# The head of a two-layer diffusion step: another order for its loads, its statistics and its first weight tiles

## The chip, the cores and the metric

The kernel runs on one core of a Trainium2 chip. Five engines work side by side, each with its own queue in program order: TensorE (PE; its weight loads are shown apart as PEld), VectorE (DVE), ScalarE (ACT), GpSimd (POOL) and SyncE (SP), which issues every DMA here. The metric is the device time of one execution in microseconds (us), the median of several runs; the profile and the trace come from one further execution.

## The reference

Two groups of 128 tokens (context and latent) of width 1024 go through the same two layers. Each layer is a half-step feed-forward, a token mixer and another half-step feed-forward. What matters here is the start of the first one, where for each group a conditioning vector gives a shift and a scale:

```
mod = silu(cond) @ w_ada[l] + b_ada[l]          # 9 vectors of 1024: shift, scale, gate, ...
h   = rmsnorm(x, g[0]) * (1 + mod[1]) + mod[0]  # rmsnorm: x * rsqrt(mean(x*x) + eps) * g
g, u = split(h @ ffn_w_in[l, 0], 2)             # 1024 -> 2 x 2816
x   = x + 0.5 * mod[2] * ((silu(g) * u) @ ffn_w_out[l, 0])
```

Everything is computed to nearly fp32 accuracy.

## The kernel before

**Layout.** Activations lie transposed: 8 slices of 128 channels (`KD` = 8) by 256 tokens (`NT`, both groups). A matrix product of fp32 accuracy is made from three faster ones: each weight tile and each operand is split into a rounded high part and the rest, and `mm3` adds high x high, high x rest and rest x high. A weight tile is 128 x 1024 fp32 (0.52 MB) in HBM, loaded into one of four `raw` buffers; `emit_hi` (ScalarE, a cast) and `emit_lo` (VectorE, a subtraction) split it; the load that reuses its buffer waits for `emit_lo`. The first five tiles (`T0` = 5) put their parts into the general `big` buffers (25 of them), the later ones into five `wh` and five `wl`. A weight tile times 8 operands is 24 products.

**The operand.** The normalisation's 1/rms is a factor per token, so it is left to the evacuation of the products (`rb`, a row of 1/rms on all partitions). The operand of slice m (`feed["hs"][m]`, here *operand m*) is x times `Amod` (gain times 1 + scale; `xfeed`: two ScalarE instructions, then two on VectorE for the rest), and two further columns hold the shift: 258 columns.

**The head.** These are all instructions ahead of the loop over tiles in `ffn_in`, at the end of `backbone`. The queues are in the order of the program text; nothing reorders them. Shift and scale of slice b need *block b* of `w_ada`: 1024 x 256 fp32, two DMAs of 0.52 MB. `block_mm(b)` multiplies it with silu(cond) into the one `pa` accumulator (8 products, 16 records), and VectorE copies that out. `block_feed(b)` (here *feed b*) transposes the copy by two small fp32 products with a selector, computes shift, scale and `Amod` on VectorE, and calls `xfeed(b)`. In a loop of ten steps, step s does block s, feed s-1, and the products of operands up to s-2 with the prepared tiles that have joined:

```
for t in range(T0):
    if step < max(2, JOIN[t]):
        continue
...
    while done[t] <= step - 2:
        k = done[t]
        mm3(pre[t], ws[t][k:k + 1], feed["hs"][k:k + 1], k == 0, k == KD - 1)
        done[t] += 1
```

Ahead of the loop x is squared slice by slice on ScalarE (`xstat`), VectorE adds the squares up in `sqa`, and `norm_chain` makes `rb`: a product with ones, a multiply-add (`rsv`), a power on GpSimd (`rsr`), a diagonal matrix on VectorE, a product with ones, a copy. Tiles 0 to 2 use the three main accumulators (`pm`), tiles 3 and 4 the two halves of `spare`. The sixth tile of the weight stream is the first that `ffn_in` multiplies itself; it takes the accumulator of tile 0, the seventh that of tile 1, once VectorE has evacuated them into `wide`.

**Loads.** SP issues in program order: the conditioning vectors, x (1.05 MB), constants (0.13 MB), parameters (0.14 MB), then weight tiles and blocks in turn. A DMA whose buffer is still read waits in SP's queue, and all behind it with it.

**Order further on.** The wrappers of the engines keep a rough clock for each (`Pace`), by which the side work of later stages (adaLN streams, attention, scans) is put between the products. In the head no such choice is made but for the norm's chain.

Of the kernel before, what the change touches and what calls it, by code (L numbers as in the profile page):

```python
# [13 lines left out]
ALU = mybir.AluOpType  # L14
# [26 lines left out]

ADA_DEPTH = 2
T0 = 5
JOIN = (0, 0, 3, 4, 5)
RAW_BUFS = 4
WH_BUFS = 5
WL_BUFS = 5
# [30 lines left out]
BR_LESS = (0, 0, 0, 0, 1, 1, 1, 1)  # L78
WO_LESS = (0, 0, 0, 0, 1, 1, 1, 1)
FO_LESS = (0, 0, 0, 0, 1, 1, 1)  # L80
LOADS = (2, 3, 4, 4)
PRE = 2
AHEAD = ("", "hl", "h", "lh", "")
T_SIDE = 3
T_SETUP = 6
YCUT = ((0, 2), (2, 2), (4, 2), (6, 2))
# [338 lines left out]
def backbone(ctx: ExitStack, tc: tile.TileContext, seq, wst, wada, wa0, wrow, xT_d, cT_d, cB_d, ck_d, cv_d, h0_d, prm_d, cst_d,  # L425
# [71 lines left out]
    def C(name):  # L497
        return cst[:, CST[name][0]:CST[name][1]]
# [59 lines left out]
    def misc(gen):  # L558
        add(gen, True)
# [5 lines left out]
    def load(out, src):  # L565
        nc.sync.dma_start(out=out, in_=src)
        pace.op("dma", out.free_size() * P * 4 / 360e3, [out], [])
# [215 lines left out]
    def rstd_diag(acc, scale, more=None):  # L783
        ps = ps1(2)
        for g in range(2):
            T_.matmul(ps[:, g:g + 1], lhsT=acc[:, g * P:(g + 1) * P], rhs=C("ones")[:, 0:1], start=True,
                      stop=more is None)
            if more is not None:
                T_.matmul(ps[:, g:g + 1], lhsT=more[:, g * P:(g + 1) * P], rhs=C("ones")[:, 0:1], start=False, stop=True)
        r = rstd_cols(ps, 2, scale)  # L790
        drop("s1", ps)
        dg = t1k()
        for g in range(2):
            V.tensor_scalar(out=dg[:, g * P:(g + 1) * P], in0=C("ident"), scalar1=r[:, g:g + 1], scalar2=None, op0=ALU.mult)
        return dg
# [867 lines left out]
    def ssd_norm(l, yv, yh, yl, box):  # L1663
# [25 lines left out]
            V.scalar_tensor_tensor(out=box["ts"][m], in0=box["ts"][m], scalar=1.0, in1=rb[:, :NT], op0=ALU.add, op1=ALU.mult)  # L1689
        box["done"] = True  # L1690

    load(cT, cT_d)
    load(x, xT_d)
    load(cst[:, 0:CST_E], cst_d[:, 0:CST_E])
    load(prm[0], prm_d[0, :, 0:PRM_R])
    V.memset(silc, 0.0)
    V.memset(halfc, -0.5)
    S.activation(out=silc[:, :, 0:2], in_=cT, func=AF.Silu)
    blocks = []

    def block_load():
        blocks.append([big(), big()])
# [3 lines left out]
    def split():  # L1706
        emit_hi()
        emit_lo()

    for n in LOADS[:-1]:  # L1710
        load_more(n)
        block_load()
    load_more(LOADS[-1])
    feed_open(0, 0)
    for m in range(KD):
        xstat(m)()
    box = {"rb": None}
    misc(norm_chain(box))
    split()
    split()  # L1720
    settle(lambda: box["rb"] is not None)
    evs = {}

    def block_mm(b):
        ps = pada()
        for k in range(KD):
            j = k % 4
            T_.matmul(ps[32 * j:32 * j + 32, :], lhsT=silc[:, k, :], rhs=blocks[b][k // 4][:, j * NT:(j + 1) * NT],
                      start=(k < 4), stop=(k >= 4))
        evs[b] = t1k()  # L1730
        V.tensor_copy(evs[b], ps)
        blocks[b] = None

    def block_feed(b):
        ev = evs.pop(b)
        pt = ps1(4)
        for h in range(2):
            T_.matmul(pt[:, 2 * h:2 * h + 2], lhsT=ev[:, h * P:(h + 1) * P], rhs=C("sel"), start=True, stop=True)
        sc = mods[0][:, 1, b, :]
        V.tensor_scalar(out=sc, in0=pt[:, 0:2], scalar1=R(0, "bada")[:, KD + b:KD + b + 1], scalar2=1.0, op0=ALU.add,  # L1740
                        op1=ALU.add)
        sh = mods[0][:, 0, b, :]
        V.tensor_scalar(out=sh, in0=pt[:, 2:4], scalar1=R(0, "bada")[:, b:b + 1], scalar2=None, op0=ALU.add)
        drop("s1", pt)
        V.tensor_scalar(out=Amod[0][:, 0, b, :], in0=sc, scalar1=R(0, "gain")[:, b:b + 1], scalar2=None, op0=ALU.mult)
        hi, lo = feed["hs"][b]
        V.tensor_copy(hi[:, NT:], sh)
        V.tensor_tensor(out=lo[:, NT:], in0=sh, in1=hi[:, NT:], op=ALU.subtract)
        xfeed(b)()

    spare = ps2()
    pre, ws = [], []
    done = {}
    for step in range(KD + 2):
        if step < KD:
            block_mm(step)
            if len(blocks) < KD:
                block_load()
                if len(blocks) == KD:
                    st["cap"] = len(seq)  # L1760
                    load_more(st["lo"] + RAW_BUFS)
        if 1 <= step <= KD:
            block_feed(step - 1)
        for t in range(T0):
            if step < max(2, JOIN[t]):
                continue
            if t == len(pre):
                ws.append(tiles8(use(("fin", 0, 0, (t % 2) * KF + t // 2))))
                pre.append(pmain(NT + 2) if t < 3 else spare[:, t - 3, 0:NT + 2])
                done[t] = 0  # L1770
            while done[t] <= step - 2:
                k = done[t]
                mm3(pre[t], ws[t][k:k + 1], feed["hs"][k:k + 1], k == 0, k == KD - 1)
                done[t] += 1
        if st["lo"] < T0 and step + 2 >= JOIN[st["lo"]]:
            split()
        if step >= KD - 3:
            for what in AHEAD[step - KD + 3]:
                what = emit_hi() if what == "h" else emit_lo()
    while st["lo"] < T0 + PRE:  # L1780
        if st["hi"] == st["lo"]:
            emit_hi()
# [54 lines left out]
```

## Time and profile before

| | |
|---|---|
| median of 3 runs | 1553.76 us (1552.73 to 1557.59) |
| profiled execution | 1555.05 us, of which the span is 1553.2 us |
| TensorE busy | 1513.9 us (97%) |
| VectorE, ScalarE, GpSimd busy | 1303.5, 864.5, 60.7 us |
| mean granted TensorE clock | 0.998 |
| HBM read, written | 342.00 MB, 4.19 MB |

The span runs from the first instruction to the last; the execution's own time also has what lies around it. Busy times are sums over an engine; a TensorE that is busy is not one at its peak, as its products overlap. All line numbers of engine work are that of the one helper which records operations (L394), so instructions are told apart by the tiles that they write and read.

### The profile page before, as it was taken

The page shows a single profiled execution, that of the slowest core. Times are in us where ns is not written, and L with a number is a line of the kernel's source. Part 1 is how long each engine was busy: PE and PEld are TensorE (multiplying, and loading weights), DVE is VectorE, ACT ScalarE, POOL GpSimd, SP SyncE. Part 2 cuts the span into 40 slices and gives each one's busy share as a digit, 9 for nine tenths or more (in the row PEclk, how much of TensorE's full clock was granted, in tenths as well). Part 3 has the DMA queues.
Part 4 walks back from the last instruction along what each step waited for, and adds up shares of the span by engine and source line. Part 5 has one row for each costly group of instructions (what it writes and reads, how often), then busy time and mean ns, then how long its engine had stood idle before and what let it go on. Part 6 is the DMA issues. An engine that isn't in the chain of part 4 may idle for free. (4 is left out here: it accounts for less than half of the span.)

```text
span 1553.2 us, 30573 instructions
## 1 busy us (share of the span) xinstructions
PE 1513.9 (97%) x11934; PEld 1421.0 (91%) x11934; DVE 1303.5 (84%) x2404; ACT 864.5 (56%) x1560; POOL 60.7 (4%) x65
## 2 busy tenths in 40 slices
PE   6999999999999999999999999999999999999997
PEld 4998889989979999899899998998897999999986
DVE  5777798986888998899989999898778989998664
ACT  3564447665576446644446544577556744665442
POOL 0000002000001000100001000110000020010000
PEclk9999999999999999999999999999999999999999
DMA  9698775553765666688766887555467568568652
GB/s 373 224 338 287 264 265 166 188 187 131 246 214 190 220 240 221 209 297 286 265 215 200 288 279 269 189 179 186 158 213 229 189 204 287 172 201 279 211 181 82
DMA packets 103345, 350.30 MB, mean 226 GB/s; under 512 B 11424, under 2 KB 19232, under 8 KB 103072
## 3 DMA queue, kind: packets, MB, share of 16 engines
q1 hardware_dynamic: 103200, 348.34, 65.9%
q8 instruction: 94, 1.54, 0.4%
q14 instruction: 51, 0.42, 0.1%
HBM read 342.00 MB, written 4.19 MB: 223 GB/s over the span
## 5 line engine op out<-in xcount | busy, mean ns | idle before, releaser
L394 PE MATMUL pm<-big,wh 128*128 128x256 f32 (+2 forms) x6568 | 1289.6, 293 | 4.3 <-DVE big L394 2.5
L394 PEld LDWEIGHTS pm<-big,wh 128*128 128x128 f32 x6568 | 1028.0, 189 | 53.3 <-issue 20.2
L394 PE MATMUL pm<-big,wl 128*128 128x256 f32 (+1 forms) x3592 | 1003.6, 281 | 0.0
L394 PEld LDWEIGHTS pm<-big,wl 128*128 128x128 f32 x3592 | 676.6, 188 | 2.3
L394 DVE TENSOR_TENSOR wl<-raw,wh 128x1024 fp32r<-128x1024 f32 x481 | 587.8, 1227 | 14.8 <-ACT wh L394 14.4
L394 ACT CAST wh<-raw 128x1024 fp32r<-128x1024 f32 x481 | 502.5, 1050 | 137.4 <-PE pm L394 87.6
L394 DVE SCALAR_TENSOR_TENSOR big<-big,big 128x1024 f32<-128x1024 f32 x198 | 241.9, 1222 | 12.8 <-DMA big<-wrow 11.4
L394 ACT CAST big<-t1k 128x256 fp32r<-128x256 f32 x88 | 36.0, 409 | 156.3 <-DVE t1k L394 156.3
L394 PE MATMUL pm<-wh,big 128*128 128x512 f32 x256 | 86.2, 401 | 2.0 <-ACT big L394 2.0
L394 ACT ACTIVATE big<-x,amod 128x128 fp32r<-128x128 f32 x96 | 33.5, 397 | 96.7 <-DVE x L394 79.1
L394 DVE TENSOR_TENSOR wide<-pm,rb 128x258 f32<-128x258 f32 (+1 forms) x108 | 45.2, 422 | 36.8 <-PE pm L394 33.3
L394 DVE SCALAR_TENSOR_TENSOR x<-pm,mods,x 128x128 f32<-128x128 f32 x152 | 43.7, 345 | 36.4 <-PE pm L394 36.2
L394 PEld LDWEIGHTS pm<-wh,big 128*128 128x128 f32 x256 | 48.2, 188 | 15.0 <-ACT big L394 2.9
L394 ACT COPY big<-pm 128x256 f32<-128x256 f32 (+2 forms) x88 | 30.8, 374 | 50.3 <-PE pm L394 50.0
L394 DVE TENSOR_TENSOR big<-t1k,big 128x256 fp32r<-128x256 f32 x128 | 55.7, 440 | 1.6 <-ACT big L394 0.9
L394 ACT ACTIVATE t1k<-wide 128x128 f32<-128x128 f32 (+1 forms) x96 | 33.6, 397 | 38.9 <-DVE wide L394 38.6
L394 PE MATMUL pm<-wl,big 128*128 128x512 f32 x128 | 50.3, 393 | 0.0
L394 PE MATMUL s<-big,big 128*64 128x128 f32 (+5 forms) x416 | 46.3, 312 | 1.5 <-ACT big L394 1.5
L394 ACT ACTIVATE t1k<-pm 128x256 f32<-128x256 f32 x58 | 22.4, 386 | 43.8 <-PE pm L394 43.8
L394 POOL TENSOR_TENSOR rsr<-rsv,halfc 128x2 f32<-128x2 f32 x9 | 6.3, 698 | 919.0 <-DVE rsv L394 919.0
L394 DVE TENSOR_TENSOR t1k<-pm,t1k 128x256 f32<-128x256 f32 x42 | 17.8, 424 | 28.6 <-PE pm L394 26.7
L394 DVE SCALAR_TENSOR_TENSOR big<-big,cw,big 128x252 f32<-128x252 f32 (+1 forms) x96 | 39.4, 485 | 2.8 <-ACT big L394 2.8
(146 smaller groups left out, 977.7 us busy)
## 6 DMA issues: line engine op xcount, KB each, us to landing
raw<-wst SPq DMA_DIRECT2D x486, 512.0 KB, 4.2
big<-wrow SPq DMA_DIRECT2D x96, 512.0 KB, 5.6
big<-wada SPq DMA_DIRECT2D x32, 512.0 KB, 5.6
big<-wa SPq DMA_DIRECT2D x16, 512.0 KB, 10.2
big<-cB SPq DMA_DIRECT2D x12, 512.0 KB, 7.4
big<-big SPq DMA_DIRECT2D x32, 64.0 KB, 5.2
x<-xT SPq DMA_DIRECT2D x1, 1024.0 KB, 4.9
big<-h SPq DMA_DIRECT2D x2, 512.0 KB, 5.2
```

The lines of the kernel that those rows point to most:

```text
L394: r = fn(*a, **k)
```

## The change

- *Loads.* Parameters and constants come ahead of x. x is loaded in four quarters, and these, the blocks and the weight tiles follow a written order (`ORDER`: w a block, x a quarter, r a weight tile): `wxrwxrwxrwx` ahead of the loop, then `wr`, `wr`, `w`, `w` behind the blocks of steps 0 to 3.
- *Zero products.* `warm(n)` puts n products of a zero tile with itself (512 columns) into the half of `spare` that tile 4 uses later: `WARM` gives 13 ahead of the loop and 9, 9, 5, 3 at the ends of steps 0 to 3.
- *Sums of squares.* ScalarE squares slices as listed in `XSTAT`; a step later TensorE sums each by two products with a column of ones into the accumulator `pq`. VectorE's additions go. The rest of the norm's chain runs at step 7 (`diag`) and step 8 (`rstd_rows`).
- *Block copies.* ScalarE copies a block's result, as its first instruction of the step.
- *Feed.* Feed s now comes in step s, behind the products, which use operands up to s-1; the loop has nine steps. Shift and scale come from one VectorE instruction in place of two. In steps 0 to 4 the split of a raw tile stands in the feed: its cast ahead of the feed, its subtraction between the ScalarE and the VectorE part of `xfeed`.
- *Tiles.* Tiles 0 to 2 join at steps 1 to 3, tiles 3 and 4 at step 8. There tile 3 first takes its seven finished operands, then `rb` is made, then all take what is left.

```
-JOIN = (0, 0, 3, 4, 5)
...
-LOADS = (2, 3, 4, 4)
 PRE = 2
-AHEAD = ("", "hl", "h", "lh", "")
+JOIN = (1, 2, 3, 8, 8)
+ORDER = "wxrwxrwxrwx wr wr w w".split()
+WARM = (13, 9, 9, 5, 3)
+XSTAT = {1: (0,), 2: (1, 2), 3: (3, 4), 4: (5,), 5: (6,), 6: (7,)}
+AHEAD = {6: "h", 7: "l", 8: "hl"}
...
+        return diag(ps, scale)
+
+    def diag(ps, scale):
         r = rstd_cols(ps, 2, scale)
...
+    zero = tmp("t512", [P, 512], F32R)
+    V.memset(zero.bitcast(F32), 0.0)
     load(cT, cT_d)
-    load(x, xT_d)
+    load(prm[0], prm_d[0, :, 0:PRM_R])
     load(cst[:, 0:CST_E], cst_d[:, 0:CST_E])
-    load(prm[0], prm_d[0, :, 0:PRM_R])
...
+    spare = ps2()
+
+    def warm(n):
+        for _ in range(n):
+            T_.matmul(spare[:, 1, :], lhsT=zero[:, 0:P], rhs=zero, start=True, stop=True)
...
-    for n in LOADS[:-1]:
-        load_more(n)
-        block_load()
-    load_more(LOADS[-1])
+    def head_load(items):
+        for c in items:
+            if c == "w":
+                block_load()
+            elif c == "x":
+                i = xs_in[0]
+                load(x[:, i:i + 2], xT_d[:, i:i + 2])
+                xs_in[0] = i + 2
+            else:
+                st["cap"] += 1
+                load_more(st["cap"])
+
+    st["cap"] = 0
+    head_load(ORDER[0])
     feed_open(0, 0)
-    for m in range(KD):
-        xstat(m)()
     box = {"rb": None}
-    misc(norm_chain(box))
-    split()
-    split()
-    settle(lambda: box["rb"] is not None)
...
-        V.tensor_copy(evs[b], ps)
+        S.copy(evs[b], ps)
...
-    def block_feed(b):
+    def block_feed(b, lo_too):
...
-            T_.matmul(pt[:, 2 * h:2 * h + 2], lhsT=ev[:, h * P:(h + 1) * P], rhs=C("sel"), start=True, stop=True)
-        sc = mods[0][:, 1, b, :]
-        V.tensor_scalar(out=sc, in0=pt[:, 0:2], scalar1=R(0, "bada")[:, KD + b:KD + b + 1], scalar2=1.0, op0=ALU.add,
-                        op1=ALU.add)
-        sh = mods[0][:, 0, b, :]
-        V.tensor_scalar(out=sh, in0=pt[:, 2:4], scalar1=R(0, "bada")[:, b:b + 1], scalar2=None, op0=ALU.add)
+            T_.matmul(pt[:, 2 - 2 * h:4 - 2 * h], lhsT=ev[:, h * P:(h + 1) * P], rhs=C("sel"), start=True, stop=True)
+        sh, sc = mods[0][:, 0, b, :], mods[0][:, 1, b, :]
+        V.tensor_tensor(out=mods[0][:, 0:2, b, :], in0=v3(pt, 2),
+                        in1=R(0, "bada").rearrange("p (i k) -> p i k", k=KD)[:, 0:2, b:b + 1].to_broadcast([P, 2, 2]), op=ALU.add)
...
-        xfeed(b)()
-
-    spare = ps2()
+        later = xfeed(b)
+        if lo_too:
+            emit_lo()
+        later()
...
-    for step in range(KD + 2):
...
+    pq = ps1(2)
+    sqs = []
+    warm(WARM[0])
+    for step in range(KD + 1):
+        if step < KD:
+            block_mm(step)
+            if step + 1 < len(ORDER):
+                head_load(ORDER[step + 1])
+                if len(blocks) == KD:
+                    st["cap"] = len(seq)
+                    load_more(st["lo"] + RAW_BUFS)
+        joined(step)
+        if step == KD:
+            mains(3, KD - 1)
+            box["rb"] = rstd_rows(dg)
+        for t in range(len(pre)):
+            mains(t, step)
+        if step > min(XSTAT):
+            while sqs:
+                m, q = sqs.pop(0)
+                for g in range(2):
+                    T_.matmul(pq[:, g:g + 1], lhsT=q[:, g * P:(g + 1) * P], rhs=C("ones")[:, 0:1], start=(m == 0 and g == 0),
+                              stop=(m == KD - 1), skip_group_check=True)
+        if step == KD - 1:
+            dg = diag(pq, 1.0 / D)
+        if step < KD:
+            for m in XSTAT.get(step, ()):
+                sqs.append((m, t1k()))
+                S.activation(out=sqs[-1][1], in_=x[:, m], func=AF.Square)
+            if step < T0:
+                emit_hi()
+            block_feed(step, step < T0)
+        if step + 1 < len(WARM):
+            warm(WARM[step + 1])
+        for what in AHEAD.get(step, ""):
+            what = emit_hi() if what == "h" else emit_lo()
```

`joined(step)` lets a tile join by `JOIN`, `mains(t, upto)` multiplies tile t with its operands below `upto`.

## Rows read from the trace of the kernel before

**Rows 1.** The page: busy time, share of the span and instructions of each engine.

```profile
PE 1513.9 (97%) x11934; PEld 1421.0 (91%) x11934; DVE 1303.5 (84%) x2404; ACT 864.5 (56%) x1560; POOL 60.7 (4%) x65
```

**Rows 2.** Stretches, core 0: us, busy of PE, PEld, DVE, ACT, POOL, granted clock, DMA.

```profile
15.00:17.00 2.00, 2.00 (x17) 0.59 (x16) 0.00 (x0) 0.37 (x1) 0.00 (x0) 1.00 1.04 420
...
6.00:37.50 31.50, 22.04 (x209) 15.46 (x210) 19.27 (x63) 11.43 (x25) 0.70 (x1) 1.00 1.03 412
...
26.87:46.00 19.13, 19.13 (x187) 16.38 (x188) 13.60 (x51) 8.28 (x18) 0.00 (x0) 1.00 0.68 266
46.00:1540.00 1494.00, 1478.69 (x11619) 1394.01 (x11618) 1273.40 (x2310) 845.68 (x1523) 59.14 (x59) 1.00 0.66 224
```

**Rows 3.** Timeline of PE's products: start, us, engine, line, out<-in, count, idle before.

```profile
15.29 1.93 PE L394 MATMUL pa<-big,silc 128*32 128x256 f32 x16
17.77 1.07 PE L394 MATMUL pa<-big,silc 128*32 128x256 f32 x16 [0.55 <-DVE t1k L394]
...
23.21 1.07 PE L394 MATMUL pa<-big,silc 128*32 128x256 f32 x16 [1.27 <-DVE t1k L394]
...
36.17 0.61 PE L394 MATMUL s<-cst,t1k 128*128 128x2 f32 x4
36.63 1.32 PE L394 MATMUL pm<-big,big 128*128 128x258 f32 x9
37.79 0.89 PE L394 MATMUL s<-big,big 128*128 128x258 f32 x6
...
45.99 0.41 PE L394 MATMUL pm<-big,wh 128*128 128x258 f32 x2
```

**Rows 4.** Timeline of PE's weight loads: those that waited for a block's DMA.

```profile
19.85 0.16 PEld L394 LDWEIGHTS pa<-big,silc 128*32 128x32 f32 x8 [0.31 <-DMA big<-wa]
...
23.62 0.18 PEld L394 LDWEIGHTS pa<-big,silc 128*32 128x32 f32 x8 [0.25 <-DMA big<-wa]
```

**Rows 5.** Groups of instructions, forms apart, 0 to 46 us: busy, mean ns, idle.

```profile
L394 DVE TENSOR_TENSOR big<-raw,big 128x1024 fp32r<-128x1024 f32 x5 | 6.0, 1223 | 1.8 <-ACT big L394 1.8
...
L394 ACT CAST big<-raw 128x1024 fp32r<-128x1024 f32 x5 | 5.1, 1035 | 0.0
...
L394 PE MATMUL s<-cst,sqa 128*128 128x1 f32 x4 | 1.0, 357 | 10.5 <-DVE sqa L394 10.5
```

**Rows 6.** Timeline, DVE and ACT, of one feed's chain.

```profile
36.81 0.35 DVE L394 TENSOR_SCALAR mods<-s,prm 128x2 f32<-128x2 f32 x2
37.07 0.22 DVE L394 TENSOR_SCALAR amod<-mods,prm 128x2 f32<-128x2 f32 x1
37.20 0.16 DVE L394 CAST big<-mods 128x2 fp32r<-128x2 f32 x1
37.33 0.70 ACT L394 ACTIVATE big<-x,amod 128x128 fp32r<-128x128 f32 x2 [3.76 <-DVE amod L394]
...
37.77 0.65 DVE L394 SCALAR_TENSOR_TENSOR big<-x,amod,big 128x128 fp32r<-128x128 f32 x2 [0.21 <-ACT big L394]
```

**Rows 7.** Timeline of the norm's chain.

```profile
12.63 0.15 DVE L394 TENSOR_SCALAR rsv<-s 128x2 f32<-128x2 f32 x1
...
13.60 0.48 DVE L394 TENSOR_SCALAR t1k<-cst,rsr 128x128 f32<-128x128 f32 x2 [0.82 <-POOL rsr L394]
...
14.14 1.22 PE L394 MATMUL s<-t1k,cst 128*128 128x256 f32 x2 [2.63 <-DVE rb L394]
```

**Rows 8.** Timeline behind the head: evacuations, a subtraction, the seventh tile's start.

```profile
45.15 0.42 DVE L394 TENSOR_TENSOR wide<-pm,rb 128x258 f32<-128x258 f32 x1
...
47.34 1.23 DVE L394 TENSOR_TENSOR wl<-raw,wh 128x1024 fp32r<-128x1024 f32 x1 [0.64 <-ACT wh L394]
...
48.48 0.42 DVE L394 TENSOR_TENSOR wide<-pm,rb 128x258 f32<-128x258 f32 x1
...
48.95 0.30 PEld L394 LDWEIGHTS pm<-big,wh 128*128 128x128 f32 x2
```

**Rows 9.** DMA issues, 0 to 50 us: KB each, median us to landing.

```profile
cT<-cT SPq DMA_DIRECT2D x1, 8.0 KB, 1.6
```

More of the change, by code (lines that the diff above doesn't have):

```diff
@@ L1698, in backbone @@
     S.activation(out=silc[:, :, 0:2], in_=cT, func=AF.Silu)
+    spare = ps2()
+    def warm(n):
+        for _ in range(n):
+            T_.matmul(spare[:, 1, :], lhsT=zero[:, 0:P], rhs=zero, start=True, stop=True)
     blocks = []
+    xs_in = [0]
     def block_load():
@@ L1737, in block_feed @@
         for h in range(2):
-            T_.matmul(pt[:, 2 * h:2 * h + 2], lhsT=ev[:, h * P:(h + 1) * P], rhs=C("sel"), start=True, stop=True)
-        sc = mods[0][:, 1, b, :]
-        V.tensor_scalar(out=sc, in0=pt[:, 0:2], scalar1=R(0, "bada")[:, KD + b:KD + b + 1], scalar2=1.0, op0=ALU.add,
-                        op1=ALU.add)
-        sh = mods[0][:, 0, b, :]
-        V.tensor_scalar(out=sh, in0=pt[:, 2:4], scalar1=R(0, "bada")[:, b:b + 1], scalar2=None, op0=ALU.add)
+            T_.matmul(pt[:, 2 - 2 * h:4 - 2 * h], lhsT=ev[:, h * P:(h + 1) * P], rhs=C("sel"), start=True, stop=True)
+        sh, sc = mods[0][:, 0, b, :], mods[0][:, 1, b, :]
+        V.tensor_tensor(out=mods[0][:, 0:2, b, :], in0=v3(pt, 2),
+                        in1=R(0, "bada").rearrange("p (i k) -> p i k", k=KD)[:, 0:2, b:b + 1].to_broadcast([P, 2, 2]), op=ALU.add)
         drop("s1", pt)
-        V.tensor_scalar(out=Amod[0][:, 0, b, :], in0=sc, scalar1=R(0, "gain")[:, b:b + 1], scalar2=None, op0=ALU.mult)
+        V.scalar_tensor_tensor(out=Amod[0][:, 0, b, :], in0=sc, scalar=1.0, in1=R(0, "gain")[:, b:b + 1].to_broadcast([P, 2]),
+                               op0=ALU.add, op1=ALU.mult)
         hi, lo = feed["hs"][b]
@@ L1748, in block_feed, with joined @@
         V.tensor_tensor(out=lo[:, NT:], in0=sh, in1=hi[:, NT:], op=ALU.subtract)
-        xfeed(b)()
-    spare = ps2()
+        later = xfeed(b)
+        if lo_too:
+            emit_lo()
+        later()
     pre, ws = [], []
     done = {}
-    for step in range(KD + 2):
[L1755 to L1763, printed above, removed]
+    def joined(step):
         for t in range(T0):
-            if step < max(2, JOIN[t]):
+            if step < JOIN[t]:
                 continue
@@ L1770, in backbone, with mains @@
                 done[t] = 0
[L1771 to L1779, printed above, removed]
+    def mains(t, upto):
+        while done[t] < upto:
+            k = done[t]
+            mm3(pre[t], ws[t][k:k + 1], feed["hs"][k:k + 1], k == 0, k == KD - 1)
+            done[t] += 1
+    pq = ps1(2)
[34 more added lines that the diff above has]
+            what = emit_hi() if what == "h" else emit_lo()
     while st["lo"] < T0 + PRE:
```

## Prediction

> **What bounds the kernel now.** I read the page's busy line first, then the stretches, then the head in order of time. TensorE (PE) is busy for 97% of the span [rows 1]. From 46 us to 1540 us it is busy for 1478.7 of 1494 us [rows 2], so what the change can move lies ahead of 46 us: the head, which ends when the first product of the sixth weight tile starts, at 45.99 us [rows 3]. Whatever that moment moves by, the end should move by. (The Pace clocks that order later side work are started in the head too; but by the fourth pair of tiles, when the side streams join, every queue waits for PE's buffers, so I count no reordering.)
>
> In the head two things bind in turn. The DMA engines are full from 6 to 37.5 us, at 412 GB/s [rows 2]: 8.39 MB of adaLN blocks, 2.62 MB of weights, 1.05 MB of x and 0.28 MB of small tables. The second halves of blocks 2 and 3 end a DMA wait of PE at 19.85 and 23.62 [rows 4]. From 26.87 to 46 PE is busy throughout [rows 2]: by then it has more to do than DMA holds back, and block 7, which by its bytes lands near 33.8, is multiplied only later.
>
> **The change, part by part.** *Bytes.* The order becomes parameters, constants, then block, quarter of x, raw weight tile, in turn. Nothing is added. Through block 3 the old order had moved 8.14 MB (x, small tables, five weight tiles, four blocks); the new one has moved the same 8.14 MB (x, small tables, three tiles, five blocks) through block 4. So block 4 lands at 23.6 by the same row [rows 4], and at 412 GB/s raw tile 3 (0.52 MB more) at 24.9, block 5 27.4, raw 4 28.7, blocks 6 and 7 at 31.2 and 33.8. SP stays ahead: raw 4 waits for raw 0's split near 11 us, block 7's buffers for block 0's products, both long past. The smaller tables first cost the start 0 to 0.3 us.
>
> *Zero products.* 13, 9, 9, 5, 3 of them sit in PE's queue up to step 3, each 512 columns. The sixth tile's 24 products of 258 columns run from 45.99 to 48.95 [rows 3, 8], 0.12 us each; 512 columns then cost 0.24, or 0.48 if slow: 3.1 to 6.2 us ahead of block 0 (lands at 7), 2.2 us in gaps of 3 to 4 us between blocks. The last three end near 25, ahead of an operand that PE has to wait for until 27.9, so they cost nothing. What they buy is the early clock: block 0's 16 products took 1.93 us, block 1's 1.07 [rows 3], though the granted clock's row reads 1.00 (2.4 GHz) in that stretch too [rows 2]. But up to step 3 DMA sets the pace, so those 0.9 us buy nothing.
>
> *Sums of squares.* Seven vector adds go; fourteen more products of fp32 columns come. The nearest row is the feed, also two fp32 products with a 128-column stationary operand: 36.17 to 36.63, 0.46 us [rows 3]. The same pair of the old norm took 1.01 with PE just woken [rows 5]. Bounds 0 and 1.01; I take 0.45 a pair because PE is awake. Nothing hides those of steps 3 to 7: they stand between the operand products and the next feed.
>
> *The chain per step.* Before, a block is fed one step after its products, and operand products come another step later, so the vector chain lies under PE work. After, at step s PE does block s, products with operand s-1, squares, feed s. The chain from feed to finished operand is long: feed at 36.17, shift and scale from 36.81, ScalarE 37.33, last vector piece 37.77 + 0.65 = 38.42 [rows 3, 6], 2.25 us. One vector instruction goes, 0.13 by the spacing of the rows; I take 2.1. PE's one block (1.0) covers part, then it waits. Period: 2.1 + 1.0 (eight of nine products, 36.63 to 37.79 being 1.16 for nine [rows 3]) + 0.45 = 3.55, against 2.55 between the last blocks. Taking the copies out of VectorE's queue removes its 0.42 us waits, but ScalarE's queue is in order too: a copy now stands behind the split of a raw tile that has not landed, and behind the last step's scaling.
>
> Step 3: ScalarE waits for raw 3, 24.9, then casts 1.03; VectorE subtracts 1.22 [rows 5] ahead of operand 3's last pieces, 0.65: operand 3 is ready at 27.9, with PE waiting from 26.0. Step 4: products to 28.9, two pairs to 29.8, feed 4; 0.65 and four small instructions, 0.6, to 31.05; raw 4's subtraction 1.22; 0.65: operand 4 at 32.9. Products and one pair: feed 5 at 34.35. Two periods: feed 6 at 37.9, feed 7 at 41.45.
>
> *The last operand.* At step 7 the norm's chain stands in VectorE's queue ahead of operand 7: from 12.63 to 13.60 + 0.48 = 14.08 [rows 7], 1.45, most of it the wait for POOL's power. From 41.55 that is 43.0; the operand's own chain then ends at about 44.4. The fourth tile's 21 products cover this: 41.9 + 2.5 = 44.4. So this part works, to within 0.3 us either way. Then the row for 1/rms, 0.5 (bounds 0.46, the feed, and 1.22, two records on a waking PE [rows 7]); twelve products, 1.45; all 24 of the fifth tile, 2.9. Sixth tile: 49.25, against 45.99: **+3.3 us**.
>
> *One wait behind.* Seven tiles are split ahead, but the eighth's cast is now not done in the head. Before, the second accumulator was evacuated at 48.48, and PE took it at 48.95 after the first had gone at 45.15 [rows 8]; in front of it stand two subtractions, the later ending 47.34 + 1.23 [rows 8]. After, operand 7 ends at 44.4, two subtractions and the first evacuation follow to 48.2, activation 0.7, two casts to 51.1, subtraction 1.2, evacuation 0.4: 52.7, where PE asks at 52.15. Between 0 and 0.7; I take 0.5. **Sum +3.8 us.** The profiled execution's own time is 1555.05, span and 1.85 around it; it would be 1558.9. The median of the runs is 1.3 below that execution, so I predict 1557.6, +0.24%. A change within 0.3% can hardly be told from none here.
>
> *A rule against it.* From 6 us on, pieces of 0.5 MB together kept 412 GB/s [rows 2]. The Trainium skill ("DMA: Bandwidth & Descriptors", section Bandwidth) advises pieces of at least 1 MiB, with 341 GB/s for one of 1 MB and 138 for one of 64 KB, measured there from GpSimd's queue. By its lower figure x in quarters would take up to 7.6 us in place of 2.5, an estimate that makes the sum +8.9. No row here has a 256 KB piece; the rate with several in flight speaks against the rule, and the sum above needs nothing of it (its mechanism is the third rival).
>
> **Rivals.**
> 1. *The cover works throughout; the gain shows.* If operands were always ready, PE's work from 25.0 on is four blocks 4.0, four feeds 1.8, five pairs 2.25, the row 0.5, 93 products at 0.122, 11.35: 44.9, that is 1.1 us sooner; with the wait behind, about 1553.2. For it: VectorE loses eight copies and seven adds. Against it: raw 3 lands at 24.9 whatever VectorE does. It decides if feed 5 starts before 31 us. It also shows how little the head can give: a gain of 4.7 us (0.3%) isn't there.
> 2. *The clock falls in the new waits (slower).* PE waits near 26 to 27.9 and 31.1 to 32.9, having only 0.12 us products between. Block 0 shows the price of a slow array, 1.93 against 1.07, a factor of 1.8. Between 28 and 35 PE does some 4 us of work on the path; at that factor it costs 3.2 more: about 1561. For it: the zero products end at 25, ahead of both waits. Against: VectorE's waits left PE idle for 1.27 us before 23.21 and its block's 16 products still took 1.07 [rows 3]. It decides if the granted clock falls below 1.00 (2.4 GHz) after 26 us. The Trainium skill ("TensorE: Matmul & The Clock Gate", Part 1) calls the slow clock the default, which activity lifts; the 1.93 and 1.07 agree, no row here shows it falling in the head.
> 3. *Quarter pieces of x don't overlap (slower).* If each paid a landing of its own, 1.6 us as the 8 KB load [rows 9], raw 3 would land 6.4 us later and the end with it: +10, about 1564. It decides if the moved rate between 6 and 25 us is under 350 GB/s. Against: the 412 GB/s.
>
> **How the numbers follow.** Forecast 0.60 (most of it within 0.3%, some 0.13 above, since 4.7 is only 0.9 us beyond its sum); cover works 0.22 (0.04 faster by more than 0.3%, should the later order of work shift too); clock 0.13; pieces 0.05 with 0.04 beyond. Slower 0.13 + 0.12 + 0.04 = 0.29, faster 0.04, same 0.67. The range runs from 1552 (the first rival, a run's spread below) to 1561 (the second's mark): about 0.12 is left out. The forecast's own is 1556 to 1559.5, by a pair at 0.35 or 0.55, the row, the wait and the start.
>
> **What would show it.** Block 4's landing at 23.6, full DMA from 6 us; operand 3 waiting for ScalarE's cast of raw 3 at 26; TensorE waits of 1.9 and 1.7 us near 26 and 31, and 0.5 to 0.7 at steps 6 and 7; feeds 5, 6, 7 at 34.3, 37.9, 41.4; no wait after the fourth tile; sixth tile at 49.2; granted clock 1.00. I'm wrong if blocks land more than 1 us off these times, if a pair costs under 0.2 us, if the chain of a feed is under 1.5 us, or if the two traces part again behind 60 us.

## The result and the profile after

The changed kernel takes **1564.45 us** in the median of 4 runs (1563.62 to 1564.96), the kernel before beside it 1553.24 (1552.56 to 1557.59): ratio 1.0057, 95% interval [1.0036, 1.0078] (the two medians alone give 1.0072). It is slower by 11.2 us; 1557.6 had been predicted, with 1561.0 as the range's upper end. The profiled execution took 1563.62 us, its span 1561.8, the mean granted clock 0.994.

The page's busy line of the kernel after (as [rows 1]) and its stretches (as [rows 2]):

```profile
PE 1534.3 (98%) x12001; PEld 1436.6 (92%) x12001; DVE 1296.6 (83%) x2382; ACT 866.2 (55%) x1568; POOL 60.5 (4%) x65
```

```profile
6.00:37.50 31.50, 27.61 (x214) 19.04 (x213) 11.44 (x35) 12.84 (x28) 0.00 (x0) 0.91 1.03 407
26.87:46.00 19.13, 17.35 (x132) 12.78 (x124) 6.43 (x22) 7.89 (x18) 0.00 (x0) 0.73 0.66 262
5.00:32.20 27.20, 23.35 (x192) 16.00 (x194) 9.18 (x28) 11.46 (x24) 0.00 (x0) 1.00 1.02 404
32.30:42.40 10.10, 10.05 (x61) 7.20 (x58) 3.41 (x13) 2.77 (x8) 0.00 (x0) 0.51 0.69 274
42.50:53.70 11.20, 11.02 (x97) 10.10 (x97) 5.67 (x19) 4.83 (x11) 0.70 (x1) 1.00 0.19 55
```

DMA is as full as before from 6 to 37.5 us, 407 against 412 GB/s. The new thing is the seventh figure, the granted clock: 0.73 from 26.87 to 46 us where it was 1.00 [rows 2]. The last three stretches cut it near its edges: full until about 32 us (a row from 32.1 to 32.2 reads 0.50 already), 0.51 (the level of 1.2 GHz) for the next ten, full again. "Busy" does not show this: a slow TensorE is as busy as a fast one, 10.05 of 10.10 us.

TensorE's products of the kernel after, in order of time (as [rows 3]):

```profile
8.66 0.64 PE L396 MATMUL pa<-big,silc 128*32 128x256 f32 x8 [0.55 <-DMA big<-wa]
...
26.71 1.07 PE L396 MATMUL pa<-big,silc 128*32 128x256 f32 x16
28.52 0.39 PE L396 MATMUL pm<-big,big 128*128 128x258 f32 x1 [0.75 <-ACT big L396]
29.71 1.23 PE L396 MATMUL pm<-big,big 128*128 128x258 f32 x8 [0.80 <-DVE big L396]
...
32.12 1.93 PE L396 MATMUL pa<-big,silc 128*32 128x256 f32 x16
33.99 2.72 PE L396 MATMUL pm<-big,big 128*128 128x258 f32 x9
36.50 1.70 PE L396 MATMUL s<-cst,t1k 128*128 128x1 f32 x8
38.13 1.93 PE L396 MATMUL pa<-big,silc 128*32 128x256 f32 x16
39.99 2.30 PE L396 MATMUL pm<-big,big 128*128 128x258 f32 x9
...
43.05 1.07 PE L396 MATMUL pa<-big,silc 128*32 128x256 f32 x16
44.30 1.60 PE L396 MATMUL pm<-big,big 128*128 128x258 f32 x9 [0.18 <-ACT big L396]
45.73 0.95 PE L396 MATMUL s<-cst,t1k 128*128 128x1 f32 x8
46.55 2.76 PE L396 MATMUL s<-big,big 128*128 128x258 f32 x21
49.14 0.59 PE L396 MATMUL s<-t1k,cst 128*128 128x256 f32 x2
...
53.90 0.40 PE L396 MATMUL pm<-big,wh 128*128 128x258 f32 x2
...
57.29 0.47 PE L396 MATMUL pm<-big,wh 128*128 128x258 f32 x2 [0.35 <-DVE wide L396]
```

Read the 16 products of a block (`pa`) as a clock of their own: 1.07 us at 26.71, 1.93 at 32.12 and 38.13, 1.07 again at 43.05. The two new waits stand ahead of the fall, 0.75 and 0.80 us, for operand 3. One square's pair and a feed cost 1.70 us at half clock, 0.95 at full. The sixth tile starts at **53.90** against 45.99 [rows 3]: +7.9. (Some expectations below say 53.77 and 52.45, where the tile's first weight load starts; here it is always its first product.) One wait behind it costs 0.5 (57.29, where 56.7 would be the end of 24 products).

ScalarE and VectorE of the kernel after, same view (as [rows 5 to 7]):

```profile
26.83 1.04 ACT L396 CAST big<-raw 128x1024 fp32r<-128x1024 f32 x1 [1.25 <-DMA raw<-wst]
...
30.62 1.05 ACT L396 CAST big<-raw 128x1024 fp32r<-128x1024 f32 x1 [1.57 <-DMA raw<-wst]
...
33.96 0.61 DVE L396 SCALAR_TENSOR_TENSOR big<-x,amod,big 128x128 fp32r<-128x128 f32 x2
...
46.27 0.16 DVE L396 TENSOR_SCALAR rsv<-s 128x2 f32<-128x2 f32 x1 [1.64 <-PE s L396]
...
48.47 0.65 DVE L396 SCALAR_TENSOR_TENSOR big<-x,amod,big 128x128 fp32r<-128x128 f32 x2 [0.20 <-ACT big L396]
```

The casts of raw tiles 3 and 4 waited for their DMA until 26.83 and 30.62; the forecast had them land at 24.9 and 28.7, so both are **1.9 us late**. Operand 4 is finished at 34.57, 1.7 behind the forecast; the norm's chain starts at 46.27, 4.7 behind. For most of the time between those two the clock was at half; run 1 shows what that is worth.

Behind the sixth tile the order of instructions is the same in both kernels on TensorE, and the trace's end stands at +8.6 us. The other 2.6 us to the medians' 11.2 lie between executions of one kernel: that of before which was profiled stood 1.8 above its median, that of after 0.8 below.

### The profile page after: what moved, and what is told of

Read it like the earlier page. It is cut to its first block, busy times and chain, and to the rows that moved or that the text cites. A ratio compares the mean times of both kernels' runs of the same rounds, so it can differ in the third digit from the quotient of the medians.

```text
span 1561.8 us, 30699 instructions
## 1 busy us (share of the span) xinstructions
PE 1534.3 (98%) x12001; PEld 1436.6 (92%) x12001; DVE 1296.6 (83%) x2382; ACT 866.2 (55%) x1568; POOL 60.5 (4%) x65
## 4 chain that ended last, share of the span: by engine, by line
PE 70%; issue 13%; DVE 9%; DMA 4%; ACT 2%; POOL 1%; SPq 1%; DVEq 0%; POOLq 0%; ACTq 0%
PE pm L396 64%; PE s L396 5%; DVE big L396 3%; DVE wl L396 3%; DVE t1k L396 2%; PE pa L396 1%; DMA big<-wa 1%; ACT big L396 1%; DMA big<-wrow 1%; DMA big<-big 1%; DMA big<-wada 1%; POOL osr L396 1%; DMA raw<-wst 1%; ACT wh L396 1%; DMA nk<-big 0%
## 5 line engine op out<-in xcount | busy, mean ns | idle before, releaser
L396 PEld LDWEIGHTS s<-big,big 128*128 128x128 f32 (+2 forms) x416 | 35.0, 172 | 6.8 <-ACT big L396 2.8
```

What stands on the lines that cost most here:

```text
L396: r = fn(*a, **k)
```

## Experiments

All are variants of one of the two kernels. "To the sixth tile" is the time from the cast of raw tile 3 to the sixth tile's first product: it takes the loads out, as far as raw tile 3 is what the head waits for. It is 27.07 us in the kernel after; the prediction's working gives 49.25 - 24.9 = 24.35.

**1. Keep TensorE at work in the new waits.** The kernel after, with more zero products between a block's and an operand's:

```
+FILL = {4: 8, 5: 6, 6: 3, 7: 3}
...
             block_mm(step)
...
         joined(step)
+        warm(FILL.get(step, 0))
```

> The changed kernel with 8, 6, 3 and 3 more zero products at steps 4 to 7, between the block's products and the operand's. In the changed kernel the granted clock was at half from 32.3 to 42.5 us and the sixth tile started at 53.77 us. If the fall of the clock is a cause, it stays at 1.00 from 5 us on, step 5's block takes 1.07 us again in place of 1.93, and the sixth tile starts 2 to 3 us sooner, near 51. If the lateness comes from the chain of each step alone and the clock only shows it, the sixth tile starts at 53.5 or later, since PE has more in its queue.

1562.31 us, ratio 1.0052 [1.0036, 1.0068]. The same stretch and products with these fillers:

```profile
32.30:42.40 10.10, 10.10 (x101) 8.05 (x101) 4.03 (x17) 3.51 (x11) 0.00 (x0) 1.00 0.73 291
```

```profile
29.00 2.11 PE L397 MATMUL s<-t 128*128 128x512 f32 x8
30.94 1.23 PE L397 MATMUL pm<-big,big 128*128 128x258 f32 x9
...
37.78 1.07 PE L397 MATMUL pa<-big,silc 128*32 128x256 f32 x16
...
41.53 1.07 PE L397 MATMUL pa<-big,silc 128*32 128x256 f32 x16
...
52.57 0.40 PE L397 MATMUL pm<-big,wh 128*128 128x258 f32 x2
```

The clock holds at 1.00, every block takes 1.07 us, and two blocks lie 3.75 apart (a period of 3.55 was forecast). Raw 3 was cast at 27.85 here, so to the sixth tile it is 24.72: holding the clock was worth 27.07 - 24.72 = **2.35 us**, net of what the fillers themselves take, and the working's 24.35 was right to 0.4. In this execution the same loads came 1.0 us later, so the sixth tile starts only 1.3 us sooner than in the kernel after; near 51 was expected. The medians part by 2.1 us with intervals that overlap, so the gain is shown by the traces and not by the totals. That the fall is no accident of one execution shows in the mean granted clock of each: 0.994 in three of the four of the kernel after and 0.996 in one, 0.996 to 0.998 in the five here.

**2. The fillers at step 4 alone,** to see which wait lets the clock fall; the code of run 1 with

```
-FILL = {4: 8, 5: 6, 6: 3, 7: 3}
+FILL = {4: 8}
```

> The changed kernel with eight more zero products at step 4 alone, between block 4 and the products with operand 3. Theory A (the wait for operand 3 near 26 to 28 us is what lets the clock fall at 32 us): the clock then holds past 32 us and blocks 5 and 6 take 1.07 us, or it falls only after the later waits (34 us or behind), sixth tile 52.2 to 52.8. Theory B (the wait of step 5 or the sum of the waits lets it fall): clock at half within 1 us of 32.25 again, sixth tile 53.5 to 54. Time 1562 to 1564 in either.

1562.95 us, 1.0061 [1.0047, 1.0075]. Two products, and two stretches:

```profile
32.94 1.07 PE L397 MATMUL pa<-big,silc 128*32 128x256 f32 x16
...
37.38 1.75 PE L397 MATMUL pa<-big,silc 128*32 128x256 f32 x16
```

```profile
28.00:35.00 7.00, 6.39 (x62) 4.72 (x50) 3.64 (x9) 3.95 (x10) 0.00 (x0) 1.00 1.03 413
...
36.60:40.20 3.60, 3.60 (x30) 2.48 (x29) 1.21 (x6) 1.39 (x4) 0.00 (x0) 0.64 0.77 302
```

With the wait of step 4 filled the clock passes 32 us at full and falls later, behind the wait of step 5, for a shorter stretch; to the sixth tile 25.54. So each of the two waits can let it fall.

**3. No zero products at all** in the kernel after.

```
-WARM = (13, 9, 9, 5, 3)
+WARM = (0, 0, 0, 0, 0)
```

> The changed kernel without any zero product. If they only lift the clock early, where DMA sets the pace, block 0 takes 1.9 us in place of 1.28, and the rest depends on when the clock falls again: with it at full up to 32 us the sixth tile starts within 0.5 us of 53.8; if the steps up to 4 now run slow as well, 1 to 4 us later. If the zero products themselves delay PE (13 to 3 in its queue), it starts sooner than 53.3.

1569.01 us, 1.0089 [1.0070, 1.0109]: the four first blocks take 1.94 to 2.27 us, the clock is full from 26.9 to 33.6 only, and 0.51 from 33.8 to 43.9. Sixth tile at 55.93, 2.0 later than with them. Nearly all of that is there at raw tile 3's cast, 28.75 against 26.83; from it to the sixth tile it is 27.18 against 27.07. The cast no longer waits for its DMA, it stands behind a square in ScalarE's queue:

```profile
28.43 0.42 ACT L396 ACTIVATE t1k<-x 128x256 f32<-128x256 f32 x1 [2.54 <-issue]
28.75 1.03 ACT L396 CAST big<-raw 128x1024 fp32r<-128x1024 f32 x1
```

That square starts at 25.17 in the kernel after. So the zero products are worth some 2 us of head, by the steps up to 3, but do not reach as far as the new waits.

**4. Sums of squares back on VectorE**, with the fillers of run 1:

```
-                for g in range(2):
-                    T_.matmul(pq[:, g:g + 1], lhsT=q[...], rhs=C("ones")[:, 0:1], ...)
+                if m:
+                    V.tensor_tensor(out=acc, in0=acc, in1=q, op=ALU.add)
```

> The changed kernel with the waits filled as in e1_fill, and the squares added on VectorE, a step late, in place of products with ones. From the cast of raw tile 3 to the sixth tile e1_fill took 24.6 us (27.85 to 52.45). If the five pairs of steps 4 to 7 lie on the path of each step, as the prediction has it at 0.45 each, this takes 22.1 to 22.6. If the waits for the operand take up what the pairs leave, it takes 24.2 or more.

1559.93 us, 1.0032 [1.0022, 1.0041]. Raw 3 is cast at 27.36, the sixth tile starts at 50.15: 22.79, 1.93 less than run 1. Five pairs stand in the steps behind that cast, 0.39 each: they do lie on the path, at about the forecast's 0.45.

**5. The copies on VectorE again**, with the fillers of run 1.

```
-        S.copy(evs[b], ps)
+        V.tensor_copy(evs[b], ps)
```

> The changed kernel with the waits filled as in e1_fill and the block copies back on VectorE. The chain from the cast of raw tile 3 to the sixth tile took 24.6 us in e1_fill. If the copy's place in ScalarE's queue costs nothing, because the operand waits are longer, it stays within 0.3 us of that; if the copy behind the cast or the scaling is what feeds wait for, it falls by 0.5 us or more. Behind 500 us e1_fill's products were further apart than those of the kernel before, 1.9 us in sum: if ScalarE's copies bring that about, it goes away here; if any other order of the head does, it stays.

1560.77 us, 1.0038 [1.0025, 1.0050]; to the sixth tile 24.56 against 24.72. Which engine copies does not matter on this path. The wider spacing behind 500 us that the expectation asks about stays, some 2 us in sum as in run 1, so it does not come from ScalarE's copies alone.

**6. The other way round: the kernel before with copies on ScalarE.**

```
-        V.tensor_copy(evs[b], ps)
+        S.copy(evs[b], ps)
```

> The kernel before with one edit, the copy of each block's result on ScalarE in place of VectorE. TensorE waited for these copies for 0.55, 1.27 and 0.50 us at 17.8, 23.2 and 26.9 us. If that is what held the head, the sixth tile starts 1 to 2.3 us sooner than 45.99. If DMA holds those blocks anyway (block 3's second half came at 23.62), it starts within 0.4 us of 45.99.

1558.51 us, 1.0028 [1.0016, 1.0041], with the sixth tile at 45.87. TensorE's waits for VectorE's copies are gone, and block 3 waits for its DMA instead:

```profile
23.83 0.64 PE L394 MATMUL pa<-big,silc 128*32 128x256 f32 x8 [0.50 <-DMA big<-wa]
```

So in this head a faster copy buys nothing: DMA sets the pace, as [rows 4] said. Yet the total rises by 4.4 us. Compared product by product with the control's trace (before against itself, run 11), its products behind 500 us lie slightly further apart: on average 118.4 ns from start to start against 117.7, which sums to some 5 us over the 7000 or so that follow each other closely; see the end of the next section.

**7. The fourth tile's older operands in the waits,** ahead of the products with the newest; the fifth tile covers the last operand. No zero products are added to the kernel after.

```
-JOIN = (1, 2, 3, 8, 8)
+JOIN = (1, 2, 3, 4, 8)
...
+        if len(pre) > 3:
+            mains(3, step - 1)
         if step == KD:
-            mains(3, KD - 1)
+            mains(4, KD - 1)
```

> The changed kernel without further zero products, but with the fourth tile joining at step 4 and multiplying its older operands ahead of the products that wait, and the fifth tile as the cover of the last operand. If real products in the waits hold the clock as zero products do, it stays at 1.00 and from the cast of raw tile 3 to the sixth tile it takes 22 to 23 us in place of the changed kernel's 26.9 and e1_fill's 24.6. If they are too few for that, the granted clock falls near 32 us again and it takes 24.5 or more.

1562.68 us, 1.0049 [1.0032, 1.0066]. Real products keep the clock at full as zeros do. Raw 3 cast at 27.99, sixth tile at 51.77: 23.78 (22 to 23 was expected), of which 1.20 is a new wait:

```profile
51.77 0.52 PE L396 MATMUL pm<-big,wh 128*128 128x258 f32 x2 [1.20 <-DVE wide L396]
```

TensorE now comes too early for the accumulator that VectorE has still to evacuate.

**8. The loads.** Three orders. The kernel after with x in one piece ahead of the tables:

```
-ORDER = "wxrwxrwxrwx wr wr w w".split()
+ORDER = "wrwrwrw wr wr w w".split()
...
-    load(prm[0], prm_d[0, :, 0:PRM_R])
+    load(x, xT_d)
     load(cst[:, 0:CST_E], cst_d[:, 0:CST_E])
+    load(prm[0], prm_d[0, :, 0:PRM_R])
```

> The changed kernel with x in one piece ahead of constants and parameters, as before the change, and the same order of blocks and tiles behind. In the changed kernel raw tile 3 was there at 26.8 us, 1.9 us later than the bytes at 412 GB/s gave. If the lateness is that of the small tables first and of the quarters, raw 3 is there near 25 and the sixth tile starts 1 to 2 us sooner than 53.77. If it comes from blocks and tiles in turn, it stays at 26.5 to 27.

1566.02 us, 1.0074 [1.0052, 1.0097]. It missed: block 0 then comes later, the first zero products are over before it, the clock is 0.51 from 10.4 to 17.1 and from 37.7 to 44.4 us, and the sixth tile starts at 56.02. Raw 3 is cast only at 29.35, again behind a square in ScalarE's queue (29.03), though the bytes had come as before the change: 290 GB/s over the first 10 us, where it is 294 before and 255 after. With the fillers of run 1, and x whole where its first quarter stood (`wxrwrwrw wr wr w w`):

> The changed kernel with the waits filled as in e1_fill, and x in one piece at the place of its first quarter. If pieces of 256 KB slow the transfers, raw tile 3 is there 0.5 us or more sooner than e1_fill's 27.8; if not, within 0.4 us of it, and the late data come from the start and from how late a landing is told.

1562.93 us, 1.0045 [1.0028, 1.0063]: raw 3 cast at 26.59, sixth tile at 52.38. By the letter of the expectation the cast is sooner (1.26 than run 1's), but it is only 0.24 sooner than the kernel after's own 26.83, and the bytes start no faster (257 GB/s over the first 10 us). It buys nothing, since block 4 starts at 27.81 as it does in run 1 (28.00), so that to the sixth tile it is 25.79. With the fillers, and the tables (p) behind block 0 (`wpxrwxrwxrwx wr wr w w`):

> The changed kernel with the waits filled as in e1_fill, and parameters and constants behind block 0 in place of ahead of it. In e1_fill block 0 was complete at 8.3 us and raw tile 3 at 27.8. If the small tables at the start hold the queue back, block 0's second half is there 0.5 to 1 us sooner and raw 3 at 26.5 to 27.2. If not, raw 3 stays at 27.5 or later; the sixth tile follows raw 3 at 24.6 us in either case.

1563.70 us, 1.0054 [1.0035, 1.0072]: raw 3 cast at 27.14, sixth tile at 51.89. That is in the range expected of tables that hold the queue back, but runs with one and the same order of loads cast raw 3 between 26.83 and 27.99 (runs 1, 2, 4, 5, 7 and the kernel after), so neither tables nor quarters are shown to be what makes the data 1.9 us late. What DMA had moved by a moment tells more. Stretches of the kernel after, then of the kernel before:

```profile
0.00:10.00 10.00, 6.25 (x31) 4.03 (x31) 0.77 (x3) 1.87 (x3) 0.20 (x4) 1.00 0.78 255
0.00:24.90 24.90, 21.15 (x147) 14.35 (x147) 7.63 (x24) 9.28 (x19) 0.20 (x4) 1.00 0.93 348
```

```profile
0.00:10.00 10.00, 0.00 (x0) 0.00 (x0) 2.84 (x8) 5.40 (x12) 0.20 (x4) 1.00 0.80 294
0.00:24.90 24.90, 9.94 (x90) 5.59 (x91) 11.13 (x33) 9.41 (x19) 0.91 (x5) 1.00 0.93 366
```

By 24.9 us the kernel after had moved 348 x 24.9 = 8.67 MB, 0.44 MB less than the one before; at 412 GB/s that is 1.1 us, and most of it is there by 10 us. (In the control's execution the kernel before had moved 8.94 MB, so some of this is chance.) The rest is order: 8.66 MB lie in the written order up to and with raw 3, as many bytes had come by 24.9, and yet raw 3 was awaited until 26.83. So bytes of later loads had come ahead of its last ones.

**9. Thirteen zero products at the start of the kernel before.**

```
+    for _ in range(13):
+        T_.matmul(spare[:, 1, :], lhsT=zero[:, 0:P], rhs=zero, start=True, stop=True)
```

> The kernel before with thirteen zero products at its start and nothing else. Its block 0 took 1.93 us at 15.3 and the granted clock rose at 17.5. If early zero products alone gave something, block 0 takes 1.07 and the sixth tile starts 0.5 to 0.9 us sooner than 46.0 to 46.4. If the clock is down again by 15 us, since PE has little between, or if DMA sets the pace behind, it stays within 0.4 us.

1558.99 us, 1.0024 [1.0008, 1.0040]; sixth tile at 46.93. They did not help the first blocks. A stretch, and block 0:

```profile
9.50:19.60 10.10, 5.64 (x38) 2.62 (x38) 4.28 (x10) 1.82 (x3) 0.70 (x1) 0.51 1.03 415
```

```profile
15.57 1.94 PE L394 MATMUL pa<-big,silc 128*32 128x256 f32 x16
```

The clock, full once the zero products had run, falls again in the wait for x's statistics, ahead of block 0.

**10. Before, with the norm's chain finished behind the loop.** Block 0 no longer stands behind it.

```
-    settle(lambda: box["rb"] is not None)
     for step in range(KD + 2):
...
+    settle(lambda: box["rb"] is not None)
```

> The kernel before, in which only the remaining links of the norm's chain are finished behind the block loop's other work of the step instead of ahead of the loop, so that block 0 need not stand behind them in TensorE's queue. Theory A (the head's end is set by DMA up to block 4 and then by TensorE's own work, the norm's chain only delays blocks that TensorE catches up with): the sixth tile starts within 0.4 us of the control's 46.39, time 1553 to 1556. Theory B (the norm's chain at the start holds TensorE back for good, up to 3 us): sixth tile near 43.5, time 1550 to 1553. Theory C (any edit of the head costs 2 to 4 us in wider spacing of the products far behind it): sixth tile as in A or B, time 3 us above what the head alone gives, 1556 to 1558.

1565.52 us, 1.0075 [1.0060, 1.0091], far from any expectation. Block 0 starts 4.5 us sooner than the control's, at 11.15, and the last operand's products still end at 46.8 (the control's sixth tile starts at 46.39): this head's pace is set by DMA and TensorE's own work. How much the earlier start alone is worth stays open, since the first four blocks took 1.93 to 2.28 us each here, where the control's second to fourth took 1.07 to 1.11. But the norm's chain now stands bare at the end:

```profile
46.78 0.50 PE L394 MATMUL s<-cst,sqa 128*128 128x1 f32 x4
...
48.84 0.70 PE L394 MATMUL s<-t1k,cst 128*128 128x256 f32 x2 [1.55 <-DVE rb L394]
...
50.46 0.80 PE L394 MATMUL pm<-big,wh 128*128 128x258 f32 x2 [0.93 <-DVE wide L394]
```

```profile
50.40:56.40 6.00, 5.94 (x27) 5.94 (x28) 4.72 (x11) 3.69 (x7) 0.00 (x0) 0.50 0.53 166
```

Around two waits of 1.55 and 0.93 us, on a TensorE that had worked without a pause from 21.8 us, the clock falls, for over 6 us. It is a fall like that of the changed kernel, with no zero product near it. With ScalarE's copies added to it:

> The run with the norm's chain finished later, and the block copies on ScalarE. Theory A (DMA and TensorE's own work set the end): sixth tile within 0.5 us of 46, and the total as that of the run with ScalarE's copies alone, 1558.5, if its 3.6 us came with the copies. Theory B: sixth tile near 43, total 1551 to 1556.

1565.38 us, 1.0076 [1.0054, 1.0098], sixth tile at 53.17, the same picture.

**11. Before, with the parameters loaded ahead of the constants,** and before against itself:

```
-    load(cst[:, 0:CST_E], cst_d[:, 0:CST_E])
     load(prm[0], prm_d[0, :, 0:PRM_R])
+    load(cst[:, 0:CST_E], cst_d[:, 0:CST_E])
```

> The kernel before with the parameters loaded ahead of the constants, nothing else: an edit that should move nothing in the head. Theory A (the wider spacing of products behind 500 us and the 2 to 4 us that medians stand above the shift of the head come from what the change does): sixth tile within 0.4 us of 46.39, time within 1 us of the control, increments of the product spacing near 0. Theory C (any other order of the start, however harmless, costs 2 to 4 us later on): sixth tile the same, time 1556 to 1558.

> The kernel before, unchanged, against itself. The head's first edit alone (block copies on ScalarE) left the sixth tile at 45.87 us and still measured 1.0028. If that is how far one measurement of one program may stray, this ratio lies off 1.000 by as much, and this second trace parts from the first by 1 to 4 us behind 400 us. If the ratio is 0.999 to 1.001 and the two traces agree within 1 us, the copies cost something later that is still unnamed.

1555.33 us, 1.0007 [0.9990, 1.0023], and 1554.79 us, 0.9999 [0.9984, 1.0015]; sixth tile at 46.38 and 46.39. A harmless edit of the head costs nothing clear of noise (the interval reaches to 3.6 us), and its products keep the control's spacing.

**12. What the runs point to, together:** the kernel after with the edits of runs 4 (without its fillers) and 7, raw 3 ahead of block 4, and splits further ahead.

```
-ORDER = "wxrwxrwxrwx wr wr w w".split()
+ORDER = "wxrwxrwxrwx rw wr w w".split()
-AHEAD = {6: "h", 7: "l", 8: "hl"}
+AHEAD = {6: "hl", 7: "h", 8: "lh"}
```

> What the runs so far gave, together: the changed kernel with the squares on VectorE (worth 2.0 us from raw 3's cast to the sixth tile), the fourth tile's older products in the waits (2.2 us, and the clock held), raw tile 3 ahead of block 4, and raw tiles 5 and 6 split one step sooner. If these add up, raw 3's cast is at 25.5 to 26.5 and the sixth tile 20 to 21 us behind it, at 46 to 47: no slower than before, within 0.1%, and not faster. If the waits they leave are filled by others, it starts at 48 or later, and the time is 0.2% or more above.

1559.39 us, 1.0027 [1.0014, 1.0041]. Raw 3 is cast at 24.22, raw 4 at 30.61, and the sixth tile starts at 49.54: 4.4 us better than the changed kernel's, still 3.2 behind the control's. The parts did not add up: from cast to sixth tile it is 25.3 us, where 20 to 21 were expected. Raw 4 comes no sooner than in the kernel after, and the clock, which was to hold, falls once more. Products, and two stretches:

```profile
32.31 0.38 PE L396 MATMUL pm<-big,big 128*128 128x258 f32 x1 [0.62 <-ACT big L396]
33.50 1.23 PE L396 MATMUL pm<-big,big 128*128 128x258 f32 x8 [0.81 <-DVE big L396]
...
41.91 0.61 PE L396 MATMUL s<-cst,sqa 128*128 128x1 f32 x4 [0.93 <-DVE sqa L396]
...
42.82 4.64 PE L396 MATMUL s<-big,big 128*128 128x258 f32 x24
```

```profile
30.00:42.00 12.00, 9.65 (x95) 7.05 (x94) 6.96 (x23) 5.50 (x13) 0.00 (x0) 1.00 0.81 323
...
43.10:46.40 3.30, 3.30 (x18) 3.30 (x17) 2.03 (x10) 1.63 (x3) 0.40 (x1) 0.52 0.30 117
```

It is at 0.52 from 43.1 us, behind a wait of 0.93 for VectorE's sums of squares, and 24 products take 4.64 us where the sixth tile's 24 took 2.96 before. The waits of 0.62 and 0.81 near 32 us, much like the two of the changed kernel, left it at 1.00 until 42. No variant beats the kernel before.

## Why the prediction was wrong

Its steps from 24.9 to 49.25 against the 53.90 measured: **+4.65 = 1.93 (late data) + 0.37 (working) + 2.35 (clock)**, from 26.83 - 24.9, 24.72 - 24.35 and 27.07 - 24.72.

- **The clock: the step that failed.** "The last three end near 25, ahead of an operand that PE has to wait for until 27.9, so they cost nothing", with a granted clock of 1.00 to the end. The wait for operand 3 came, 0.75 and 0.80 us for the 1.9 of the forecast, and the second rival with it: the clock was at 0.51 from 32.3 to 42.4 us. (The wait of 1.7 at the next step does not show, as block 5 at half clock fills it; with the clock still full it is 0.18 and 0.87 in run 2.) This rival was given 0.13 because of one row, block 3's 1.07 us behind a wait of 1.27 [rows 3]. One wait survived is no rule: runs 1 and 2 show that filling the waits keeps the clock, run 10 that longer ones drop it in the other kernel too, run 12 that waits like these need not drop it. What decides between them is not shown. The rival's price was 3.2 us for the 2.35 measured, and it looked for the slow stretch from 28 us, 4 us too soon. The Trainium skill ("TensorE: Matmul & The Clock Gate", section "HAM oscillation — how this bites in real kernels") describes such a case: waits of several us for DMA, between short groups of products, return the array to its slow clock. The trace agrees as to the fall (0.51 behind the waits) and differs in the waits, which are of 0.75 and 0.80 us; I had weighed only the skill's sentence on the default.
- **The data: a term mis-sized.** "The smaller tables first cost the start 0 to 0.3 us" is the working's only term for later data, and it came to 1.9 at raw 3: some 1.1 of a slower start and 0.8 of later loads' bytes ahead of raw 3's (run 8). The lateness is there from the first block, whose second half was awaited until 8.66 where I had 7; landings more than 1 us off were one of my own signs of being wrong. From 6 to 37.5 us the rate is the forecast's (407 for 412), but the order by bytes holds only to about 1 us. The third rival (pieces of x that don't overlap, +6.4 at raw 3) is refuted by the rate from 6 to 25 us, 404 where its mark was under 350; that its 1564 is nearest to the measured 1564.45 is luck. The trace does not bear out the Trainium skill's advice of 1 MiB pieces ("DMA: Bandwidth & Descriptors", section Bandwidth) here either: by the estimate from its figures the quarters would have cost 5.1 us more. Which part of the new order slows the start is open.
- **What held.** The chain per step (24.35 against 24.72 at full clock), the pairs (0.45 against 0.39), the cover of the last operand (it is ready at 48.47 + 0.65 = 49.12, and the fourth tile's products give way at 49.14), the 0.5 us wait behind the sixth tile, and the first rival's refutation: raw 3 sets operand 3, whatever VectorE does (run 5). Two readings beside the sum did not hold. That "those 0.9 us buy nothing", of the early zero products, is answered by run 3: without them raw 3's cast is 1.9 us later. And the 2.55 us "between the last blocks" of the kernel before was misread, its last two start 3.44 apart (35.17 and 38.61).
- **Head and total: open.** "Whatever that moment moves by, the end should move by" is right in the trace to 0.7 us (+7.9 and +8.6) and too simple for the medians. Nearly every altered head ends some us further back than its sixth tile moved: run 4 +3.8 in the head, +5.0 by its ratio (0.32% of 1554), run 6 -0.5 and +4.4, run 9 +0.5 and +3.7, run 12 +3.2 and +4.2. The two runs under 11 speak against this being the price of any edit. One part is a slightly wider spacing of the later products, some 2 to 5 us in all in most of these traces and 2 in the kernel after, none in run 9's nor in run 11's. Another is that one profiled execution may stand 3 us from its kernel's median (run 9: 1555.76 and 1558.99). Executions of one kernel differ in their granted clock, and a lower one goes with a longer time: of the 81 executions of the kernel before that ran beside the experiments, the 29 with a mean clock of 0.998 have a median of 1552.8 us, the 7 with 0.994 or 0.995 one of 1558.1. Run 9's ten have 0.990 to 0.996, run 12's mostly 0.994 to 0.996; run 6's, with 0.997 and 0.998, owe nothing to it. No run isolates the cause of either part. The forecast of 1557.6 carried over where one execution stood to its median: of the 6.9 us that the median missed it by, 4.8 lie between the two profiled executions (+8.6 for +3.8) and 2.1 in where each stands to its own median.

## What to carry to other kernels

Zero products keep TensorE's clock only as far as they reach: ask of each new wait behind them what the granted clock does there, and put work (real products, where there are any) into the wait itself. That one trace has a wait which left the clock at full says little about the next. A feed moved one step closer to its use turns the cover of a step into a wait; price it with the clock at half as well as at full. Where DMA sets a head's pace, an engine's faster copy buys nothing (run 6), but a slow TensorE can still hold up the queue that the data wait for (run 3).

## What the hardware showed

- A row of granted clock 1.00 need not mean fast products where no change of the clock has been recorded yet: from 15 to 17 us it reads 1.00 [rows 2] while block 0 took 1.93 us [rows 3]. With thirteen zero products ahead of it (run 9) the same block took the same 1.94 us and the row reads 0.51. The duration of a known group of products is the better clock.
- The fall can come behind the waits and not in them: in the changed kernel they end at 29.71 us and the clock drops near 32, with TensorE at work in between, so the slow block is not the one that waited. (In run 9 it falls within a long wait.)
- Like waits need not end alike: 0.75 and 0.80 us stood ahead of ten us at half clock in the changed kernel, 0.62 and 0.81 left it at full for 8 us in run 12, and so did 1.27 in the kernel before [rows 3].
- Products can lie on average 0.7 ns further apart between two kernels whose order of instructions there is the same, with the granted clock at full in both (run 6: some 5 us over 7000 products). The cause is not known.
